# Weight-summing transfers in pairs behind eight of the attention's weight tiles, instead of one behind each of 30 tiles and two in the next stage

## The chip, the core and the metric

One core of a Trainium2 chip runs the kernel. The core has five engines, each with an in-order queue of its own: TensorE (PE in the profile; its weight loads are PEld), VectorE (DVE), ScalarE (ACT), GpSimd (POOL) and SyncE (SP). Sixteen DMA engines move data between the large memory and the core's on-chip memory; SP issues almost all transfers of this kernel and POOL the ones that this change moves. The metric is the time of one execution on the device in microseconds (us), lower is better; the median over several runs counts.

## What is computed

One layer over 512 latent tokens of width 1024 with 256 context tokens. A modulated norm, one wide input projection, and from its columns two mixers side by side: a bidirectional Mamba-2 SSD scan with 32 heads in 4 groups, and windowed attention with 16 query heads on 4 key heads. Both are projected, gated and merged, and a gated ConvFFN follows.

```python
h_lat = modulate(x, norm1_g, sh1, sc1);  p_lat = h_lat @ w_in
y_l = ssd_bidir(...)                      # chunks of 128 tokens, both directions
att_lat = window_ctx_attention(q, k, v, k_ctx, v_ctx, sink)
out = (g_ssd * (ssd @ w_o_ssd) + g_att * (att @ w_o_att)) @ w_out
x = x + gt1 * out
u = dwconv_centred(modulate(x, norm2_g, sh2, sc2) @ w_up, ...)
x = x + gt2 * ((silu(u[:, :D_FF]) * u[:, D_FF:]) @ w_down)
return rmsnorm(x, final_g)
```

All is float32. Each product of matrices is made of three faster ones: both operands are split into a high part and a low part (a rounded copy and the rest), and high by high, high by low and low by high are added up.

## The kernel before

**Stages.** In order: modulation and the first projections (until about 88 us of the profile), attention (to about 366), the SSD scan (to about 700), the output projections, the ConvFFN. PE runs matmuls in all of them.

**Weight tiles.** A weight tile is 128 x 1024 (512 KB). `load_raw` (L172) lets SP load it into one of three `raw` buffers (tile `wraw` in the profile). It is then split: ACT copies it rounded into `whi`, DVE subtracts into `wlo`; of each there are two buffers. In `split` (L178, L179) this is done for the stages that go through `run`, which loads one tile ahead. In the attention it is done by `high` (L1078) and `low` (L1081) inside `product_atoms`: a planner orders the attention's work, and beside the attention proper 30 weight tiles (the list `BESIDE`, numbered g from 0) are multiplied to fill PE: query and key projections, gates `z` of the SSD (written away at L1118), and parts of the attention's output projection (L1067 to L1069, written away at L1109). `high` of tile g also issues the load of tile g + 1, which waits until the split of the tile that held the buffer is done.

**Queries and keys.** A query tile is made into the operands of the scores by `q_low` (L878, L880): the low part lands in a `tc` buffer (two in all, shared with `out_low` at L1003), and three transfers of SP copy half-tiles within the on-chip memory. The last waits for the first. Scores are at L948; for each block ACT takes exponentials (L964), PE transposes (L984), ACT and DVE split (L988, L992), PE multiplies by the values (L997).

**Start of the SSD stage.** The attention's end also makes decay tables. They are written to the large memory (`cs_d`, `tt_d`) and read back spread over all partitions: `tb` (L1241), from which ACT makes `eT` (L1286), and `fb` (L1565, 512 KB each, eight per group of heads, four buffers), from which ACT makes `E` (L1584). The stage's own weight tiles have key `x`. The first gives BT after a short convolution (L1381 on ACT, L1382 and L1383 on DVE, L1389 on ACT, L1390 on DVE), and PE transposes BT at L1409 after it has multiplied the second tile.

**The weight sums.** The ConvFFN's last product works with sums of blocks of `w_down`. They are made ahead of time by transfers alone: `SUMS` is a list of 32 transfers of 704 KB (tile `dsum`), from the large memory to itself, four plain copies and then four that add to what the copies wrote, and this four times over; two of the four copying groups read what an earlier group summed. `sum_step` (L155 to L160) issues the next one from POOL and makes it wait for the DVE instruction that it is given, the low part of a split. It is called for every tile of the attention by `low` (L1079 to L1081) and, while the list lasts, for the `x` tiles by `load` (L198 to L200). POOL's other work in the attention is nil; its first work of the SSD stage comes after 425 us. The sums are read in the ConvFFN only.

Of the kernel before, what the change touches and what calls it, by code (L numbers as in the profile page):

```python
# [13 lines left out]
ALU = mybir.AluOpType  # L14
# [25 lines left out]
def raw(ap):  # L40
    return ap.bitcast(F32)
# [3 lines left out]
def tile_hybrid_layer(  # L45
# [31 lines left out]
    V, S, G, T = nc.vector, nc.scalar, nc.gpsimd, nc.tensor  # L77
# [69 lines left out]
    SUMS = []  # L147
# [4 lines left out]
        SUMS += [(DSUMS[j][q], more[q], dict(accum_op=ALU.add, max_dma_last_dim=DK * P)) for q in range(4)]  # L152
    BEHIND = mybir.DependencyInfo(mybir.DependencyClass.Sync, mybir.DependencyReason.DATA)

    def sum_step(ins):  # L155

        if SUMS:
            o, x, how = SUMS.pop(0)
            dma = G.dma_start(o, x, **how)  # L159
            tc.add_manual_dep(dma.ins, ins.ins.name, BEHIND, reason="weight sums behind a split")  # L160
# [3 lines left out]
    def load_raw(key):  # L164
        a, n = src[key]
        if key[0] == "dn" and key[1] >= 4 and key[1] % 2:
            if "dnraw" not in F:
                F["dnraw"] = hpool.tile([P, 5, 6 * P], F32, tag="hlh", name="dnraw")
            r = F["dnraw"][:, key[1] // 2 % 5, :]
        else:  # L170
            r = wpool.tile([P, 1024], F32, tag="raw", name="wraw", bufs=3)
        dma = nc.sync.dma_start(r[:, :n], a)  # L172
        if key[0] == "m":
            M_LOADS[key[1]] = dma
        return r, n

    def split(r, n, hi, lo):
        S.copy(hi[:, :n], r[:, :n])  # L178
        return V.tensor_tensor(lo[:, :n], r[:, :n], raw(hi[:, :n]), ALU.subtract)  # L179
# [3 lines left out]
    def load(key):  # L183
        r, n = load_raw(key)
        if key[0] == "m":
            return r
        if key in ELSEWHERE:
            hi, lo = ELSEWHERE[key]()
            split(r, n, hi, lo)
            return hi, lo  # L190
        if key[0] == "dn" and key[1] % 4 > 1:
            if "dnw" not in F:
                F["dnw"] = hpool.tile([P, 2, 2, 6 * P], F32R, tag="hll", name="dnw")
            hi, lo = (F["dnw"][:, key[1] % 2, i, :] for i in range(2))
        else:
            hi = wpool.tile([P, 1024], F32R, tag="whi", name="whi", bufs=2)
            lo = wpool.tile([P, 1024], F32R, tag="wlo", name="wlo", bufs=2)
        low = split(r, n, hi, lo)  # L198
        if key[0] == "x":
            sum_step(low)  # L200
        return hi, lo

    def run(prog, early=None):

        seq = [k for keys, _ in prog for k in keys]
        have, nload, nuse = {}, 0, 0
        for keys, fn in prog:
            nuse += len(keys)
            ahead = 1 + (early in keys) + any(k[0] == "dn" for k in keys)
            while nload < min(nuse + ahead, len(seq)):  # L210
                have[seq[nload]] = load(seq[nload])
                nload += 1
            fn(*[have.pop(k) for k in keys])
# [102 lines left out]
    class Plan:  # L316
# [6 lines left out]
        def add(self, name, engine, cost, needs, rank, emit, whole=True, load=0.11, late=False):  # L323


            self.atoms[name] = dict(
                name=name, engine=engine, cost=cost, needs=needs, rank=rank, emit=emit, whole=whole, load=load,
                late=late, start=None,
            )
# [86 lines left out]
    with tc.tile_pool(name="spool", bufs=1) as sp:  # L416
# [235 lines left out]
        r = {}  # L652
        cq = tmp("te")[:, :LC]
        for j in range(KT):
# [46 lines left out]
            x = ("hi", "lo") if j >= NU else ("hh", "hl")  # L701
# [31 lines left out]
        for n in range(2):  # L733
            for j in range(KT):
                x = ("hi", "lo") if j >= NU else ("hh", "hl")
# [319 lines left out]
    def product_atoms(g, key, accs):  # L1055

        kind, t = key
        d, R, G_ = {}, 1e6 + 100 * g, "%d" % g
# [19 lines left out]
            S.copy(d["w"][0], d["r"])  # L1078

        def low():  # L1080
            sum_step(V.tensor_tensor(d["w"][1], d["r"], raw(d["w"][0]), ALU.subtract))  # L1081

        def rope_part(f):
            scale = -0.125 if kind == "k" else 1.0
# [37 lines left out]
        rw = R - 2e6 if g != 1 else -500  # L1122
        atom("w" + G_, "ACT", 1.05, was, rw, high, late=g > OLD)
        atom("v" + G_, "DVE", 1.225, ["w" + G_], rw, low, late=g > OLD)
        ks = range(-4 if kind == "k" else 0, 8)
        for k in ks:
# [1054 lines left out]
```

## Time and profile before

| | |
|---|---|
| median of 3 runs | 1239.54 us (1237.92 to 1241.78) |
| the profiled execution | 1237.59 us, span 1235.8 us |
| PE, DVE, ACT, POOL busy | 99%, 75%, 55%, 14% of the span |
| transfers issued by SP | 94736 packets, 181.32 MB, 46.7% of the time of 16 DMA engines |
| transfers issued by POOL (the weight sums) | 8960 packets, 23.07 MB, 8.3% |
| mean granted PE clock | 0.994 of full speed |

The span is what the profiler saw of the execution, from its first instruction to its last. Times inside the profile are counted from the span's start. A row of an order of time gives start, length, engine, line, operation, what is written from what, and in brackets how long the engine had idled and what released it. A row of waits gives who waited for whom, the sum, the number of times and the longest. "DMA to landing" is the time from the issue of a transfer to its last byte.

### The profile page before, as it was taken

What the parts mean: (1) busy time and instruction counts of PE and PEld (TensorE: products, weight loads), DVE (VectorE), ACT (ScalarE), POOL (GpSimd) and SP (SyncE); (2) the same over time, 40 slices, a digit from 0 to 9 for tenths busy, and PEclk for the clock granted to TensorE, in tenths of its full rate; (3) what the DMA queues carried; (4) which work ended last, traced back from release to release, by engine and by line L of the source; (5) the groups of instructions that cost most, each with busy time, mean ns of one, the idle gap of its engine ahead of it and who ended that gap; (6) DMA issues with size and microseconds to landing.
All of it is one profiled execution on the core that took longest, in us unless ns stands there. A gap on an engine that the chain in (4) does not pass through costs nothing.

```text
span 1235.8 us, 18429 instructions
## 1 busy us (share of the span) xinstructions
PE 1222.6 (99%) x6790; PEld 1023.5 (83%) x6790; DVE 921.5 (75%) x1518; ACT 685.8 (55%) x1289; POOL 170.6 (14%) x177
## 2 busy tenths in 40 slices
PE   9999999999998999999999999999999999999997
PEld 6798888888877877778777778889988888889997
DVE  5857788888554688697896768667777877778785
ACT  5658788787444457476575663223634344345662
POOL 0000000100110043262451631000200000000000
PEclk9999999999998999999999999999999999999998
DMA  9645585745798346346356568676133433337662
GB/s 361 259 135 185 108 219 162 155 150 139 206 244 197 107 117 164 127 124 200 97 172 197 173 206 266 229 244 208 51 108 115 136 104 117 112 106 235 186 178 82
DMA packets 104761, 206.35 MB, mean 167 GB/s; under 512 B 8928, under 2 KB 52768, under 8 KB 104416
## 3 DMA queue, kind: packets, MB, share of 16 engines
q1 hardware_dynamic: 94736, 181.32, 46.7%
q0 software_dynamic: 8960, 23.07, 8.3%
q8 instruction: 53, 0.87, 0.3%
q10 hardware_dynamic: 976, 0.79, 0.2%
q14 instruction: 36, 0.29, 0.1%
HBM read 182.54 MB, written 40.17 MB: 180 GB/s over the span
## 4 chain that ended last, share of the span: by engine, by line
PE 96%; DMA 2%; DVE 1%; ACT 1%; issue 0%; SPq 0%; POOL 0%; DVEq 0%; ACTq 0%; POOLq 0%
PE acc L230 19%; PE acc L233 19%; PE acc L231 19%; PE score L948 3%; PE po L997 3%; PE pt L984 2%; PE mis L570 2%; PE mis L1601 2%; PE mis L1494 2%; PE acc L1973 2%; PE acc L1975 2%; PE acc L1974 2%; PE mis L1609 1%; PE mis L1974 1%; PE mis L1973 1%; PE mis L1975 1%
## 5 line engine op out<-in xcount | busy, mean ns | idle before, releaser
L178 ACT CAST whi<-wraw 128x1024 fp32r<-128x1024 f32 (+3 forms) x118 | 120.0, 1018 | 151.0 <-PE acc L231 111.8
L230 PE MATMUL acc<-hlh,whi 128*128 128x512 f32 x472 | 195.0, 413 | 0.0
L179 DVE TENSOR_TENSOR wlo<-wraw,whi 128x1024 fp32r<-128x1024 f32 (+3 forms) x118 | 142.9, 1211 | 66.5 <-ACT whi L178 64.1
L231 PE MATMUL acc<-hll,whi 128*128 128x512 f32 x472 | 185.7, 394 | 0.0
L233 PE MATMUL acc<-hlh,wlo 128*128 128x512 f32 x472 | 185.6, 393 | 0.1
L230 PE MATMUL acc<-mh,whi 128*128 128x512 f32 x368 | 143.3, 390 | 0.0
L233 PE MATMUL acc<-mh,wlo 128*128 128x512 f32 x368 | 143.2, 389 | 0.0
L231 PE MATMUL acc<-ml,whi 128*128 128x512 f32 x368 | 143.2, 389 | 0.0
L233 PEld LDWEIGHTS acc<-hlh,wlo 128*128 128x128 f32 x472 | 89.0, 188 | 20.4 <-DVE wlo L179 0.8
L230 PEld LDWEIGHTS acc<-hlh,whi 128*128 128x128 f32 x472 | 89.4, 189 | 18.0 <-issue 3.1
L231 PEld LDWEIGHTS acc<-hll,whi 128*128 128x128 f32 x472 | 89.4, 189 | 17.5 <-issue 2.4
L230 PEld LDWEIGHTS acc<-mh,whi 128*128 128x128 f32 x368 | 69.1, 188 | 14.4
L233 PEld LDWEIGHTS acc<-mh,wlo 128*128 128x128 f32 x368 | 69.1, 188 | 14.4
L231 PEld LDWEIGHTS acc<-ml,whi 128*128 128x128 f32 x368 | 69.1, 188 | 14.2
L284 POOL TENSOR_TENSOR rs<-ms,phalf 128x2 f32<-128x2 f32 (+1 forms) x5 | 4.8, 954 | 463.8 <-DVE ms L283 463.8
L1382 DVE SCALAR_TENSOR_TENSOR ta<-acc,half,ta 128x511 f32<-128x511 f32 (+1 forms) x66 | 43.9, 665 | 32.7 <-ACT ta L1381 32.4
L957 DVE CUSTOM_DVE_ANT_0 p<-score,winm,nsink 128x512 f32<-128x512 f32 (+1 forms) x64 | 51.8, 810 | 15.4 <-PE score L948 13.9
L964 ACT ACTIVATE p<-p,mneg 128x512 f32<-128x512 f32 (+1 forms) x64 | 49.7, 777 | 15.4 <-DVE mneg L957 14.8
L1381 ACT ACTIVATE ta<-acc,half 128x512 f32<-128x512 f32 (+1 forms) x66 | 46.8, 709 | 19.8 <-PE acc L233 18.6
L230 PE MATMUL acc<-hch,whi 128*128 128x256 f32 x176 | 54.7, 311 | 0.0
L159 POOL DMA_DIRECT2D dsum<-wdn x24 | 20.7, 861 | 241.0 <-DVE wlo L1081 222.4
L992 DVE TENSOR_TENSOR ptl<-pt,pth 128x512 fp32r<-128x512 f32 x72 | 47.5, 685 | 8.5 <-ACT pth L988 7.7
(414 smaller groups left out, 3186.9 us busy)
## 6 DMA issues: line engine op xcount, KB each, us to landing
wraw<-wup SPq DMA_DIRECT2D x44, 512.0 KB, 3.6
dsum<-wdn POOLq DMA_DIRECT2D x24, 704.0 KB, 7.9
fb<-cs_d SPq DMA_DIRECT2D x32, 512.0 KB, 6.5
wraw<-wm SPq DMA_DIRECT2D x32, 512.0 KB, 4.0
wraw<-wx SPq DMA_DIRECT2D x24, 512.0 KB, 3.7
wm<-wm SPq DMA_DIRECT2D x16, 512.0 KB, 8.3
wraw<-wz SPq DMA_DIRECT2D x16, 512.0 KB, 4.2
wraw<-wos SPq DMA_DIRECT2D x16, 512.0 KB, 4.9
```

The costliest lines, as they stand in the source:

```text
L178: S.copy(hi[:, :n], r[:, :n])
L179: return V.tensor_tensor(lo[:, :n], r[:, :n], raw(hi[:, :n]), ALU.subtract)
L230: T.matmul(ps, wh, xh[:, k0 + k, :], start=a, stop=False)
L231: T.matmul(ps, wh, xl[:, k0 + k, :], start=False, stop=False)
L233: T.matmul(ps, wl, xh[:, k0 + k, :], start=False, stop=b)
L948: T.matmul(ps[:, o : o + len(z) * P], Q[h][:, b * P : (b + 1) * P], k[:, j, z[0] * P : (z[-1] + 1) * P], start=v == 0 and o % 512 in (0, P ...
L957: V.tensor_tensor_reduce(p[:, :w], d["ps"][i][:, o0 : o0 + w], m, op0=ALU.add, op1=ALU.min, scale=1.0, scalar=nsink[:, h : h + 1], accum_o ...
L964: S.activation(p, p, AF.Exp, bias=d["mneg"][:, i : i + 1], scale=-1.0, accum_out=d["den"][:, i : i + 1])
L992: V.tensor_tensor(d["ptl"][x], d["pt"][x], raw(d["pth"][x]), ALU.subtract)
L997: T.matmul(d["po"], vst[:, cols[x], j, :], d[y][x], start=x == 0 and y == "pth", stop=x == c - 1 and y == "ptl")
L1381: S.activation(o[:, :n], ps[:, :n], AF.Identity, scale=hcol(base_w, stride + i), bias=hcol(base_b, i))
L1382: V.scalar_tensor_tensor(o[:, 1:n], ps[:, 0 : n - 1], hcol(base_w, i), o[:, 1:n], ALU.mult, ALU.add)
```

## The change

`sum_step` can issue several transfers behind one instruction. Tiles 4 to 11 of the attention carry two each, all others one, and the `x` tiles of the SSD stage carry none: 4 + 16 + 12 = 32, so the list is used up with tile 23. No transfer is added or removed, and their order stays.

```diff
-    def sum_step(ins):
-
-        if SUMS:
+    def sum_step(ins, n=1):
+
+        for _ in range(min(n, len(SUMS))):
             o, x, how = SUMS.pop(0)
             dma = G.dma_start(o, x, **how)
             tc.add_manual_dep(dma.ins, ins.ins.name, BEHIND, reason="weight sums behind a split")
...
-        low = split(r, n, hi, lo)
-        if key[0] == "x":
-            sum_step(low)
+        split(r, n, hi, lo)
         return hi, lo
...
         def low():
-            sum_step(V.tensor_tensor(d["w"][1], d["r"], raw(d["w"][0]), ALU.subtract))
+            sum_step(V.tensor_tensor(d["w"][1], d["r"], raw(d["w"][0]), ALU.subtract), 1 + (4 <= g < 12))
```

Lines behind L200 stand two lines earlier in the kernel after.

## The prediction

> **What bounds the kernel now.** I read the engine table of the page first, then the waits of TensorE, then TensorE's order of time at its longest wait, then the chain of waits back from there.
>
> ```profile
> PE 1222.6 (99%) x6790; PEld 1023.5 (83%) x6790; DVE 921.5 (75%) x1518; ACT 685.8 (55%) x1289; POOL 170.6 (14%) x177
> ...
> PE mis L1409 <- DVE BT L1390: 4.0, 1, 4.0
> ```
>
> TensorE (PE) works for 1222.6 of 1235.8 us, so a change that removes no matmul can gain only what PE loses to waits and to a lower clock. Of its waits one is long: L1409, the first transposes of the SSD stage, waits 4.0 us for the tile BT from VectorE (DVE). PE around it:
>
> ```profile
> 379.71 0.39 PE L233 MATMUL acc<-hlh,wlo 128*128 128x512 f32 x1
> 384.10 1.12 PE L1409 MATMUL mis<-ident,BT 128*128 128x128 f32 x4 [4.00 <-DVE BT L1390]
> ...
> 388.87 0.52 PE L233 MATMUL acc<-hlh,wlo 128*128 128x512 f32 x1
> 389.23 0.39 PE L230 MATMUL acc<-hlh,whi 128*128 128x512 f32 x1
> 389.46 0.39 PE L231 MATMUL acc<-hll,whi 128*128 128x512 f32 x1
> ...
> 262.74 1.31 PE pt L984 x12
> ```
>
> Matmuls follow each other every 0.23 us at full pace (389.23 to 389.46), so the last one before the wait gives way at 379.94. From there to 389.23 there are 4 transposes and 9 matmuls to do (three rounds of L230, L231, L233). Twelve transposes take 1.31 us in the chain, 0.11 each. Undisturbed: 4 x 0.11 + 9 x 0.23 = 2.5 us. It took 389.23 - 379.94 = 9.3. **The place costs 6.8 us**: 4.16 of waiting (to 384.10), 2.64 of slow work after it. The table by stretches (stretch and its length, busy us of PE, PEld, DVE, ACT, POOL, then granted clock, DMA share, GB/s) says why the work is slow:
>
> ```profile
> 381.30:384.10 2.80, 0.00 (x0) 0.00 (x1) 2.01 (x4) 1.41 (x3) 0.00 (x0) 0.68 1.14 254
> 384.10:388.20 4.10, 4.03 (x11) 2.92 (x12) 1.95 (x3) 0.77 (x2) 0.00 (x0) 0.50 0.90 208
> ...
> 366.00:380.00 14.00, 14.00 (x74) 11.79 (x72) 1.23 (x1) 3.62 (x10) 2.03 (x2) 1.00 1.08 242
> ```
>
> The clock falls during the wait (0.68 over 381.30 to 384.10 is full clock for 1.0 us, then half, so at 382.3, 2.4 us into it) and is 0.50 until 388.2 at least. Before it, from 366 to 380, the DMA engines are full (share 1.08). The chain of waits that ends there, in order of time (start, us, what):
>
> ```profile
> 355.22 7.90 DMA tb<-tt_d
> 363.47 1.04 ACT whi L178
> ...
> 366.18 11.71 DMA fb<-cs_d
> ...
> 377.92 2.45 ACT E L1584 x8
> 380.37 0.67 ACT ta L1381
> ...
> 383.35 0.69 DVE BT L1390
> ...
> 384.88 1.22 DVE wlo L179
> ```
>
> ScalarE (ACT) is an in-order queue: the E work of the SSD's first chunk stands ahead of the convolution L1381 that BT comes from. E waits for fb, a load that needs 11.71 us to land. While it travels, ACT and DVE idle and PE uses up its lead. What fills the DMA engines are the weight sums. POOL's order of time shows their issues, two answers on line L159 the landings of the last two, and an answer on line L1565 what the later fb loads need:
>
> ```profile
> 351.69 1.07 POOL L159 DMA_DIRECT2D dsum<-wdn  x1 [5.64 <-DVE wlo L1081]
> 358.23 1.03 POOL L159 DMA_DIRECT2D dsum<-wdn  x1 [5.46 <-DVE wlo L1081]
> 366.06 1.01 POOL L159 DMA_DIRECT2D dsum<-wdn  x1 [6.81 <-DVE wlo L179]
> 369.04 1.02 POOL L159 DMA_DIRECT2D dsum<-wdn  x1 [1.97 <-DVE wlo L179]
> ...
> DMA to landing us min/median/max: 13.6/13.6/13.6
> ...
> DMA to landing us min/median/max: 15.8/15.8/15.8
> ...
> L1565 SPq DMA_DIRECT2D fb<-cs_d x27: 359/385/840, 447.6 to 690.7; - x27
> ...
> DMA to landing us min/median/max: 5.2/6.4/9.5
> ```
>
> The four last sums accumulate. Two are issued beside fb, at 366.06 and 369.04, and land after 13.6 and 15.8 us. The 27 fb loads after 395 us, with no sum about, land in 5.2 to 9.5 us, median 6.4.
>
> **The change, part by part.** On every engine the instructions keep their order; only the waits of POOL's transfers change. There are 32: four plain copies, four accumulating ones, four times over. Before, one goes behind each of the 30 attention tiles and two behind the first two tiles of the SSD stage. After, tiles 0 to 3 and 12 to 23 carry one each, tiles 4 to 11 two each: 16 + 16 = 32.
>
> *Removed at the end.* The eight transfers issued from 328.7 us on move forward; the last of the 32 now goes behind tile 23, at 325.93 before. Issued there it lands near 335 (325.93 and the 9.3 us of an accumulating one, quoted below), and from then on none is about. If fb is issued at 366.18 as now and takes the median 6.4, it lands at 372.6. BT followed the landing by 384.04 - 377.89 = 6.15 us, so it is ready at 378.7, before PE asks at 379.94. The wait goes, and with it the slow clock. The next in line is the split of the third weight tile, whose low part ended at 386.10, 2.06 us after BT: now 380.8. PE asks for it after 4 transposes and two matmuls, at 379.94 + 0.44 + 0.46 = 380.84. That fits with nothing to spare, but there is a second shift:
>
> ```profile
> 360.30 0.39 PE L1069 MATMUL acc<-khi,wlo 128*128 128x512 f32 x1
> ```
>
> fb is issued behind the fourth SSD weight load on SP's queue, that load behind the low part of the first tile's split, that behind ACT's cast (363.47), and that behind tb, a load of 128 KB that needed 7.90 us beside two sums. The cast's buffer is free when PE ends the last tile but one (row above, next tile from 360.54), so the cast can go up to 2.9 us earlier, and fb with it. Between 0 and 2.9 I need none for the forecast; whatever comes of it is spare.
>
> *Moved forward.* From tile 12 on the sequence is the old one eight places early, and of the same kind at each tile (plain for plain); the new load lies at tiles 4 to 11, where before POOL issued:
>
> ```profile
> 124.32 1.10 POOL L159 DMA_DIRECT2D dsum<-wdn  x1 [8.76 <-DVE wlo L1081]
> 137.11 1.02 POOL L159 DMA_DIRECT2D dsum<-wdn  x1 [11.69 <-DVE wlo L1081]
> ...
> 173.42 0.52 POOL L159 DMA_DIRECT2D dsum<-wdn  x1 [8.13 <-DVE wlo L1081]
> 179.53 0.50 POOL L159 DMA_DIRECT2D dsum<-wdn  x1 [5.60 <-DVE wlo L1081]
> ...
> DMA to landing us min/median/max: 9.3/9.3/9.3
> ```
>
> An accumulating one lands after 9.3 us (that of 137.11). After: two accumulating at 124.3, two at 137.1, then two plain twice (156.3 and 164.3, where accumulating ones stood), two accumulating at 173.4 and two more at 179.5 (plain before), then plain pairs at 191.8 and 200.9. The dense place is 173 to some 197: a first landing at 182.7, the next three each 5.2 us on (369.04 + 15.8 less 366.06 + 13.6), 198.3 at most. POOL has nothing else here, so its own extra waits cost nothing. What counts is which load from SP's queue is late. Weight loads, the copies that build the queries, and who needs them:
>
> ```profile
> L172 SPq DMA_DIRECT2D wraw<-wz x1: 1874/1874/1874, 177.8 to 177.8; - x1
> ...
> 198.27 1.04 ACT L1078 CAST whi<-wraw 128x1024 fp32r<-128x1024 f32 x1
> ...
> L880 SPq DMA_DIRECT2D q<-tc x1: 462/462/462, 177.3 to 177.3; - x1
> ...
> 184.85 0.58 ACT L1003 COPY tc<-po 64x512 f32<-64x512 f32 x1 [1.70 <-PE po L997]
> ...
> L880 SPq DMA_DIRECT2D q<-tc x2: 462/464/467, 198.8 to 200.0; - x2
> ...
> DMA to landing us min/median/max: 2.2/2.3/2.7
> ...
> 207.29 0.28 PE L948 MATMUL score<-khi,q 128*128 128x256 f32 x1
> ```
>
> Weight loads are issued three tiles ahead: that of 177.8 is cast at 198.27, 20 us later, so even a landing as slow as the slowest sum's 15.8 us is in time. The query copy of 177.3 holds a tc buffer that ACT writes again at 184.85: 7.5 us. The copy of 200.0 feeds the score at 207.29: 7.3 us, of which 2.7 were used. So I take 0 for the attention; the bounds are 0 and what the second and third rival cost. Below zero is out: PE is busy without a gap there (PE's only long wait is the one above).
>
> [...]
>
> **Sum.** Against the profiled execution, 1235.8 of span in 1237.59 us: -4.16 - 2.64 + 0 = -6.8, a span of 1229.0 in 1230.8 us. The median of the runs, 1239.54, lies 1.95 above that execution; I keep the distance: 1239.54 - 6.8 = **1232.7 us**. A change within 0.3% (3.7 us, so 1235.8 to 1243.3) cannot be told from none here; -6.8 is 0.55%.
>
> **The rivals.** *fb stays late by itself (0.12).* From 366.18 with the worst 9.5 it lands at 375.7, BT at 381.8: PE waits 1.9. With the clock at full, as it was 1.9 us into the old wait, the gain is 4.9, 1234.6 us; with the slow work of before as well it is 4.9 - 2.64 = 2.3, 1237.2. For it: five such loads follow at once and share the engines. Against: the first goes first. [...]
>
> *The query copies at 200 come late (0.08)*: gain and loss cancel.
>
> ```profile
> DMA to landing us min/median/max: 2.2/2.7/7.3
> ```
>
> The worst of all query copies took 7.3. The last one is issued once its forerunner (197.6) has landed: 197.6 + 7.3 + 7.3 = 212.2, 4.9 after the score wants it, with the 2.64 of slow clock 7.5: 1239.54 - 6.8 + 7.5 = 1240.2. Against: by 197 only plain copies are left, and beside those this copy took 2.7 at most.
>
> *Slower (0.14)*: the copy of 177.3 gets through only behind the queued sums at tiles 8 and 9. ACT then stands at L1003 from 184.85 until 193.1 to 198.3 (third or fourth landing), 8.2 to 13.4 us, with exponentials and transposed scores behind it on its queue and PE behind those. With 2.64 for the clock and the 6.8 gained: 1243.6 to 1248.8; it decides from a hold of 4.2 us on. For it: fb did starve beside two sums. Against: the copy is small, its worst landing (7.3) would end at 184.6, and that case had an accumulating sum over it since 164.3, which is now a plain pair, so the copy will be issued before the sums of 173.4 get going.
>
> **How the numbers follow.** Forecast 0.66 (its own range 1231.1 to 1235.0: the runs' 1237.92 to 1241.78 less 6.8), rivals 0.12, 0.08, 0.14. Faster: 0.66 and half of the first rival (the other half I leave to the lower clock), 0.72. Same: its other half and most of the second, 0.13. Slower: 0.15. The range runs from 1 us below the forecast's lower end to the second rival, 1230.0 to 1240.5, leaving out the third and a little of the rest.
>
> **What would show it.** Right: no wait of PE at L1409, clock 1.00 throughout 366 to 400, fb of the first chunk landing within 5.2 to 9.5 us, tb well under 7.9, POOL's last sum near 326 us, PE without a gap from 85 to 380. First rival: L1409 still waits, 1 to 3 us. Second: PE waits at a score near 207. Third: ACT idle at L1003 on a DMA near 185. The forecast is wrong if the wait at L1409 stays with no sum on the way, or if PE shows a new gap in the attention.

## The result, and the profile after

| | median | runs | lowest to highest | ratio to the kernel before, with its 95% interval |
|---|---|---|---|---|
| before | 1239.54 us | 5 | 1237.92 to 1241.78 | |
| after | 1232.03 us | 5 | 1229.70 to 1234.24 | 0.9936, 0.9916 to 0.9955 |
| after once more, in the third group below | 1231.58 us | 5 | 1231.35 to 1232.64 | 0.9931, 0.9917 to 0.9944 |

The kernel after is faster by 7.5 us (0.6%) where 6.8 were forecast. The profiled execution after took 1229.70 us, its span 1227.9 against 1235.8. The engine table and the waits of TensorE in it:

```profile
PE 1218.8 (99%) x6790; PEld 1021.5 (83%) x6790; DVE 921.4 (75%) x1518; ACT 686.7 (56%) x1289; POOL 170.0 (14%) x177
```

```profile
PE mis L288 <- POOL rs L282: 1.1, 1, 1.1
PE mis L446 <- DVE ones L429: 1.0, 1, 1.0
PE mis L271 <- ACT tc L2073: 0.8, 1, 0.8
```

The wait for BT, 4.0 us before, is gone (the three that are left are the same as before, near the start and the end). PE is also busy for 3.8 us less, with the same 6790 matmuls. The stretches show where most of that comes from (columns as in the prediction):

```profile
366.00:380.00 14.00, 14.00 (x77) 12.08 (x76) 5.85 (x8) 8.16 (x19) 0.00 (x0) 1.00 0.82 216
...
381.30:384.10 2.80, 2.80 (x14) 2.27 (x13) 2.01 (x4) 0.79 (x2) 0.00 (x0) 1.00 0.63 237
384.10:388.20 4.10, 4.10 (x32) 3.91 (x31) 1.88 (x3) 1.50 (x3) 0.00 (x0) 1.00 0.06 22
```

The clock is 1.00 throughout, and 384.10 to 388.20 holds 32 matmuls, most of them half as wide, where it held 11. The DMA engines are not full from 366 to 380 (0.82, before 1.08). ScalarE's order of time at the place:

```profile
357.95 0.42 ACT L1284 ACTIVATE eT<-tb 128x256 f32<-128x256 f32 x1 [1.94 <-DMA tb<-tt_d]
359.88 1.05 ACT L178 CAST whi<-wraw 128x1024 fp32r<-128x1024 f32 x1 [1.51 <-PE acc L1066]
...
368.82 2.45 ACT L1582 ACTIVATE E<-fb,TX 128x128 f32<-128x128 f32 x8 [1.85 <-DMA fb<-cs_d]
```

The first cast of the SSD stage (L178) now waits for PE and not behind tb, 3.59 us earlier than before (363.47); fb is issued earlier with it, and the E work starts at 368.82 instead of 377.92. How much of the span belongs to this place follows from two markers on PE in each execution, a score in the attention and a group of transposes (L1409, L1407 after) beyond the place. Before, then after:

```profile
203.56 0.28 PE L948 MATMUL score<-khi,q 128*128 128x256 f32 x1
...
403.00 0.60 PE L1409 MATMUL mis<-ident,tc 128*128 128x128 f32 x4
```

```profile
202.86 0.28 PE L946 MATMUL score<-khi,q 128*128 128x256 f32 x1
...
395.55 0.60 PE L1407 MATMUL mis<-ident,tc 128*128 128x128 f32 x4
```

Between them lie 199.44 us before and 192.69 after: 6.75 us. Another 0.70 lies ahead of the first marker, all of it in the first 20 us (the matmul that starts at 20.0 us before starts 0.74 us earlier after), and the remaining 0.45 of the 7.9 behind the second. The 0.70 does not need the change: the first sum of all is issued at 92.2 us in this execution of the kernel before, and between 91.3 and 92.1 in other executions of kernels that do the same up to there.

### The profile page after: what moved, and what is told of

Its sections match the earlier page's. It is cut to its first block, busy times and chain, and to the rows that moved or that the text cites. A ratio compares the mean times of both kernels' runs of the same rounds, so it can differ in the third digit from the quotient of the medians.

```text
span 1227.9 us, 18427 instructions
## 1 busy us (share of the span) xinstructions
PE 1218.8 (99%) x6790; PEld 1021.5 (83%) x6790; DVE 921.4 (75%) x1518; ACT 686.7 (56%) x1289; POOL 170.0 (14%) x177
## 4 chain that ended last, share of the span: by engine, by line
PE 99%; DVE 0%; ACT 0%; issue 0%; POOL 0%; DVEq 0%; ACTq 0%; POOLq 0%
PE acc L228 20%; PE acc L231 20%; PE acc L229 20%; PE score L946 3%; PE po L995 3%; PE pt L982 2%; PE mis L568 2%; PE mis L1599 2%; PE mis L1492 2%; PE acc L1971 2%; PE acc L1973 2%; PE acc L1972 2%; PE mis L1607 1%; PE mis L1972 1%; PE mis L1971 1%; PE mis L1973 1%
## 5 line engine op out<-in xcount | busy, mean ns | idle before, releaser
L178 ACT CAST whi<-wraw 128x1024 fp32r<-128x1024 f32 (+3 forms) x118 | 120.0, 1018 | 156.4 <-PE acc L229 112.1
L784 DVE SCALAR_TENSOR_TENSOR tm<-wraw,csil,tm 128x512 f32<-128x512 f32 x56 | 44.4, 793 | 12.4 <-DMA wraw<-wm 11.3
```

The source lines that it names most:

```text
L784: V.scalar_tensor_tensor(acc, r[:, u * 512 : u * 512 + 512], sc, acc, ALU.mult, ALU.add)
```

## The experiments

Three groups of four kernels each; the kernels of one group ran on one chip beside the kernel before (medians 1239.28, 1238.73 and 1240.47 us). Each ratio goes by the kernel before of its own group, so kernels of different groups are compared by their ratios. The first group takes the change apart.

**The last two transfers alone.** Their old places behind the first two tiles of the SSD stage are freed. To make room, the transfers behind tile 4 move forward by up to two places, so tiles 26 to 29 carry the last four, all accumulating, where tiles 26 and 27 carried plain ones before.

```diff
-            sum_step(V.tensor_tensor(...), 1 + (4 <= g < 12))
+            sum_step(V.tensor_tensor(...), 1 + (4 <= g < 6))
```

> The kernel after with pairs behind attention tiles 4 and 5 only: the list ends with tile 29, the last two transfers leave the two first tiles of the SSD stage and nothing else of the old order is kept off (two accumulating transfers still go near 351 and 358 us). Theory (fb starves beside the two transfers issued after 366 us): these two alone carry the gain; fb is issued near 366, lands after some 6 to 8 us, PE waits 0 to 0.5 us at the transposes of BT, the clock is 1.00 from 366 to 400: 1232 to 1234.5 us, ratio 0.993 to 0.996. Rival 1 (the early loads tb decide: they were late beside the transfers at 351.7 and 358.2, which are kept here): tb still needs near 8 us, PE waits 1.5 to 4 us and the time is 1236 to 1239.5. Rival 2 (the gain of the change lies in the attention's denser order or in the start of the execution, not in this place): no wait of 4 us at the place, and yet 1237 to 1239.5.

Measured: 1236.66 us (9 runs, 1233.23 to 1237.48), ratio 0.9971 (0.9960 to 0.9983). The chain of waits and PE's waits:

```profile
346.31 5.43 DMA cs_d<-du
...
351.75 6.80 DMA tt_d<-tt
...
358.62 7.93 DMA tb<-tt_d
...
366.90 1.04 ACT whi L178
...
369.60 6.46 DMA fb<-cs_d
```

```profile
PE acc L228 <- ACT whi L178: 2.2, 1, 2.2
```

fb lands in 6.46 us, as the theory wants, and yet more than half of the gain is missing. The time is lost ahead of fb: the tables are written late (cs_d, tt_d), tb is late behind them, the first cast starts at 366.90, and PE waits for that cast. Rival 1, the early loads, has both the number and the place. But the accumulating sums at tiles 26 and 27 (issued at 339.38 and 345.02, landed after 9.9 and 12.9 us; the plain ones before landed after 6.1 and 5.6) may be part of why the tables are late, so this run does more than free the last two. The next one does only that.

**The same, with the two moved behind later tiles of the SSD stage** (in the kernel before):

```diff
-        if key[0] == "x":
+        if key[0] == "x" and key[1] not in (16, 20):
```

> The kernel before with the last two transfers put behind two later weight tiles of the SSD stage instead of the first two; all 30 tiles of the attention keep one each. Theory (it is the time of those two transfers beside fb, not that they stand in the SSD stage or that others stand earlier): the wait at BT goes to under 0.5 us, 1232 to 1234.5 us. Rival 1 (tb decides): 1236 to 1239.5. Rival 3 (later loads of the SSD stage suffer in the same way, so what is gained at the first chunk is lost at the next): a new PE wait of 2 to 4 us after 390 us, 1236 to 1240.

Measured: 1233.09 us (1232.52 to 1235.17), ratio 0.9956 (0.9944 to 0.9969). Time and the wait for BT are as the theory has them; but in the profiled execution, the slowest of the five, PE waits 3.1 us for the first cast, for the same reason as in the run above (tb issued at 361.06, cast at 367.80). No new wait comes behind 390 us, so rival 3 falls.

**The earlier places alone.** Six pairs in the attention, nothing between tile 23 and the SSD stage, the last two transfers where they were.

```diff
-            sum_step(V.tensor_tensor(...))
+            sum_step(V.tensor_tensor(...), (1 + (4 <= g < 10)) * (len(SUMS) > 2))
```

> The other part of the change alone: six pairs in the attention, so that no transfer goes between tile 23 and the SSD stage, but the last two of the list stay behind the first two tiles of the SSD stage. Theory (fb starves beside those two): tb lands in 3 to 5 us, fb is issued up to 3 us earlier than before (363 to 366) but still needs 9 to 12 us, PE waits 1 to 4 us at BT and the clock may still fall: 1235 to 1239.5 us. Rival 1 (tb and the early cast decide): tb in 3 to 5 us, no wait at BT, 1232 to 1234.5. Rival 2 (the gain lies in the attention): 1232 to 1234.5 with a wait of 2 us or more still there.

Measured: 1230.90 us (1230.15 to 1231.76), ratio 0.9935 (0.9924 to 0.9947): the whole gain, with the two transfers that were to be its cause still in place. POOL's and ScalarE's order of time:

```profile
362.88 1.01 POOL L159 DMA_DIRECT2D dsum<-wdn  x1 [36.18 <-DVE wlo L179]
368.77 1.03 POOL L159 DMA_DIRECT2D dsum<-wdn  x1 [4.88 <-DVE wlo L179]
```

```profile
359.07 0.42 ACT L1286 ACTIVATE eT<-tb 128x256 f32<-128x256 f32 x1 [2.67 <-DMA tb<-tt_d]
360.28 1.05 ACT L178 CAST whi<-wraw 128x1024 fp32r<-128x1024 f32 x1 [0.79 <-PE acc L1068]
...
369.90 2.46 ACT L1584 ACTIVATE E<-fb,TX 128x128 f32<-128x128 f32 x8 [2.53 <-DMA fb<-cs_d]
```

One sum is issued just ahead of fb (362.88, fb at 363.00), the second 5.8 us later, and fb lands after 6.9 us. So "the two sums issued beside fb starve it" cannot be the whole cause. Rival 1 has the mechanism (tb after 4.5 us, no wait at BT); the time is 1.1 us below its range.

**The last two as plain copies**, at their old places. The last addition into two blocks of the sums is left out.

```diff
+    SUMS[-2:] = [(o, x, {}) for o, x, _ in SUMS[-2:]]
```

> The kernel before with the last two of the 32 transfers as plain copies: the last addition is left out of two blocks of the sums, so the output differs. Places, sizes and order stay. Theory (an accumulating transfer starves the loads, a plain copy of the same bytes hardly does): fb lands in 6 to 8 us, PE waits under 1 us at BT: 1232 to 1235 us. Rival (any transfer of 704 KB beside fb costs the same, by its bytes): fb still needs 10 us or more, the wait stays 3 to 4 us: 1238 to 1240.

Measured: 1240.33 us (12 runs), ratio 1.0011 (1.0001 to 1.0021); the wait for BT is 4.0 us. The chain of waits:

```profile
359.35 6.38 DMA tb<-tt_d
...
368.78 11.03 DMA fb<-cs_d
```

Two plain copies beside fb (issued at 368.66 and 370.09) hold it for 11.03 us, as the accumulating ones did for 11.71. That they accumulate does not decide.

These four left a new theory, the chain: the decay tables pass through four transfers in a row, written (cs_d, tt_d), tb read, fb read, and a delay in each adds up against a room of a few us. The second group tests it, and the terms that the prediction put at nothing.

**Two transfers late in the attention, none later.**

```diff
-            sum_step(V.tensor_tensor(...), 1 + (4 <= g < 12))
+            sum_step(V.tensor_tensor(...), 0 if 24 <= g < 28 else 1 + (4 <= g < 10))
```

> Six pairs at tiles 4 to 9, so 30 transfers are issued by tile 23; the last two, accumulating, go behind tiles 28 and 29 (near 351 and 358 us), as two accumulating ones did before; tiles 24 to 27 and the first tiles of the SSD stage carry none. Chain theory (formed after the first four runs: the tables go through four transfers in a row, cs_d and tt_d written, tb read, fb read, and each of them is slowed by whatever sum is then on the way): the tables are written in some 2 to 3 us, tb takes 6 to 8 us, fb 6 to 8 us; BT is late by 0 to 2.5 us: 1232 to 1235.5 us, between the kernel after and the one that only frees the first tiles of the SSD stage (1236.66). Old theory (only transfers beside fb matter): 1231 to 1233. If tb decides alone: 1235.5 to 1237.5.

Measured: 1230.14 us (1229.87 to 1230.72), ratio 0.9929 (0.9917 to 0.9942). ScalarE's order of time, and PE's only new wait:

```profile
363.34 1.03 ACT L178 CAST whi<-wraw 128x1024 fp32r<-128x1024 f32 x1
...
372.77 2.46 ACT L1582 ACTIVATE E<-fb,TX 128x128 f32<-128x128 f32 x8 [5.57 <-DMA fb<-cs_d]
```

```profile
PE acc L231 <- DVE wlo L179: 0.4, 1, 0.4
```

tb is late, the cast too (363.34, as late as before), fb starts late and lands in 6.7 us, all as the chain theory says; only the price was put too high, because the room takes it: 0.4 us of wait is left. The time lies below all three ranges and nearest to that of the old theory, so it is tb and the cast, and not the time, that speak for the chain here. E starts 3.95 us later than after (368.82) and costs almost nothing, so the room is about that large.

**Double density in the attention.** Four transfers behind each of tiles 4 to 11.

```diff
-            sum_step(V.tensor_tensor(...), 1 + (4 <= g < 12))
+            sum_step(V.tensor_tensor(...), 4 * (4 <= g < 12))
```

> All 32 transfers behind tiles 4 to 11, four behind each (none behind tiles 0 to 3), so all are issued by 201 us and POOL's queue holds up to four sums at a time. Theory (the attention has slack for loads of 10 us and more late, at twice the density of the change too): no new PE wait over 0.5 us between 90 and 366 us, 1230 to 1233 us. Rival (the query copies or weight loads come late: ACT held at L1001, or a score waits): a PE wait of 3 us or more between 125 and 230 us, 1235 to 1246.

Measured: 1234.36 us (1232.77 to 1236.32), ratio 0.9962 (0.9950 to 0.9974). It is the rival's mechanism, at less than its price (a wait of 2.3 us where it had 3 or more, and a time between the two ranges):

```profile
PE score L946 <- DMA q<-tc: 2.3, 1, 2.3
```

The last query copy (issued at 204.25, landed after 5.3 us) is late for the score, as the prediction's second rival has it. Nothing is held at L1001 (ACT's copy into `tc`, L1003 before).

**No sums in the attention at all**; they go behind the ConvFFN's first 32 tiles.

```diff
-        split(r, n, hi, lo)
+        low = split(r, n, hi, lo)
+        if key[0] == "up":
+            sum_step(low)
...
-            sum_step(V.tensor_tensor(...), 1 + (4 <= g < 12))
+            sum_step(V.tensor_tensor(...), 0)
```

> No transfer in the attention at all: the 32 go behind the first 32 tiles of the ConvFFN's first product, one each. A bound for what the sums still cost the attention and the start of the SSD stage after the change. If the attention pays nothing for them (the prediction's cost of 0): 1230 to 1233 us, the same as after. If it still pays: 1226 to 1230. If the ConvFFN has less slack for them than the attention: a new PE wait behind 900 us and 1233 to 1240.

Measured: 1233.30 us (6 runs, 1231.36 to 1235.84), ratio 0.9956 (0.9945 to 0.9968). The two markers:

```profile
203.29 0.28 PE L948 MATMUL score<-khi,q 128*128 128x256 f32 x1
...
395.97 0.60 PE L1409 MATMUL mis<-ident,tc 128*128 128x128 f32 x4
```

Between the markers lie 192.68 us without any sum and 192.69 in the profiled execution after. But the pairs (124 to 201 us) lie ahead of the first marker. A score that starts at 119.28 us before, at 118.58 after and at 119.01 here lies ahead of them: from it to the first marker all three need 84.28 us. So in these profiles neither stretch pays anything for the sums. What this kernel pays lies in the ConvFFN: against the profiled execution of before it loses 2.4 us between 900 and 1100 us; waits for three low parts make up 1.1 of them. The cause of the spread of its other runs is open.

**The clock alone.** In the kernel before, 18 matmuls whose result is not used go ahead of the transposes of BT.

```diff
+            if g == 0:
+                warm = misb()
+                for _ in range(18):
+                    tc.keep_in_program_order(T.matmul(warm, hlh[:, 0, :P], hlh[:, 0, :], start=True, stop=True))
```

> The kernel before with 18 matmuls of 128x512 put on TensorE ahead of the first transposes of BT; what they compute is not used. They take 18 x 0.23 = 4.1 us, as much as the wait, and keep TensorE busy in it, so that only the slow work after the wait goes. If the prediction's split holds (4.16 us of wait, 2.64 us of slow clock): clock 1.00 after the wait, 1236 to 1238 us. Rival (the slow clock costs nothing by itself, because BT's followers are late anyway): 1239 to 1241.

Measured: 1240.68 us (11 runs, 1237.21 to 1243.12), ratio 1.0012 (1.0002 to 1.0023); no gain. VectorE's and PE's order of time in the profiled execution (span 1235.7):

```profile
380.79 0.69 DVE L1390 SCALAR_TENSOR_TENSOR BT<-tb,ta 128x512 f32<-128x512 f32 x1 [0.76 <-ACT tb L1389]
```

```profile
381.88 4.25 PE L1439 MATMUL mis<-hlh 128*128 128x512 f32 x18
```

Here tb was late (cast at 366.08) and PE waited 1.2 us for the first cast. But fb, issued at 368.78, landed after 6.54 us, and BT was ready at 381.48, before PE came to the added matmuls. So this execution had no wait for BT that they could fill: they stand in for nothing and cost their 4.25 us. The clock is 1.00 from 384.10 to 388.20, in an execution with no wait over 1.2 us at this place. PE's busy time (1224.5 us) less the added work is 1220.2 us, 2.4 below before; that is near the 2.64 of slow work, but any execution without the slow stretch would show it. How the price splits into wait and clock therefore rests on the rows of the kernel before alone; this profile does not test it. The median lies in the rival's range, and why the other executions are no faster is open.

The third group asks whether the delays add up, and whether the pairs at tiles 10 and 11 cost something.

**Both late groups together.**

```diff
-            sum_step(V.tensor_tensor(...))
+            sum_step(V.tensor_tensor(...), 0 if 24 <= g < 28 else 1 + (4 <= g < 8))
```

> Four pairs at tiles 4 to 7, one each at the others up to tile 23, none at tiles 24 to 27, one each at tiles 28 and 29 and at the two first tiles of the SSD stage: the last four transfers of the kernel before (all accumulating) at their old places, the four ahead of them moved forward. Either half alone was free (1230.14 us with the two at tiles 28 and 29, 1230.9 us with the two in the SSD stage). Chain theory (the delays of tb and fb add up, and the room of some 4 us takes one of them but not both): tb lands late, fb too, BT late by 2 to 4 us, and the time goes back to 1236 to 1239.5 us. Rival (the queue of eight behind each other is what starves the tables; four are handled): 1230 to 1233.5.

Measured: 1238.62 us (11 runs, 1236.38 to 1239.47), ratio 0.9982 (0.9973 to 0.9991). Either half alone gave 0.993; together most of the gain is lost again. The chain of waits, and PE's wait:

```profile
350.80 3.32 DMA tt_d<-tt
354.19 7.08 DMA tb<-tt_d
...
364.32 13.68 DMA fb<-cs_d
```

```profile
PE mis L1409 <- DVE BT L1390: 4.3, 1, 4.3
```

tb is only 2.6 us slower than in the run that keeps the last two and frees the rest (7.08 against 4.5), but fb needs 13.68 us instead of 6.9, with the same two transfers issued around it. The sum of 358.02 (landed after 9.1 us) is still on the way beside the one of 364.20. So the delays do more than add up.

**Four in a row at tiles 26 to 29.**

```diff
-            sum_step(V.tensor_tensor(...), 1 + (4 <= g < 12))
+            sum_step(V.tensor_tensor(...), 0 if 24 <= g < 26 else 1 + (4 <= g < 8))
```

> Four pairs at tiles 4 to 7, none at tiles 24 and 25, one each at tiles 26 to 29 (four accumulating ones, from about 338 us on), none in the SSD stage: the same four transfers, 13 us earlier than in the run with two at tiles 28 and 29 and two in the SSD stage. Chain theory: the writes of the tables and tb are late (tb issued near 358, landed near 366), the first cast of the SSD stage is then late for TensorE by 1 to 3 us, fb itself lands in 6 to 8 us: 1232.5 to 1237 us. Rival (only what is on the way beside fb and tb counts, the two transfers ahead of them are gone by then): 1230 to 1232, as with two.

Measured: 1234.76 us (1233.83 to 1236.86), ratio 0.9956 (0.9943 to 0.9968). The chain of waits, and PE's wait:

```profile
353.07 8.72 DMA tt_d<-tt
361.87 5.61 DMA tb<-tt_d
...
367.82 1.04 ACT whi L178
```

```profile
PE acc L228 <- ACT whi L178: 3.2, 1, 3.2
```

The same four transfers some 12 us earlier hit the tables' writing instead of fb, and PE waits for the first cast instead of BT.

**Six pairs, the list done with tile 25**, and **the kernel after once more**:

```diff
-            sum_step(V.tensor_tensor(...), 1 + (4 <= g < 12))
+            sum_step(V.tensor_tensor(...), 1 + (4 <= g < 10))
```

> The kernel after with six pairs instead of eight: none at tiles 10 and 11, the list ends with tile 25 (near 338 us). Theory (the two runs with six pairs agreed within 1.6 us, the kernel after ranged over 4.5 us; its pairs at tiles 10 and 11 sometimes make the query copies near 200 us late for the score at 207 us): 1229.5 to 1231, all runs within 1.5 us. Rival (the sums near 332 and 338 us reach the tables again): 1232 to 1235.

> The kernel after once more, beside the same runs of the kernel before as the other three: 1230 to 1234 us. If the spread comes from the query copies, some profile of it shows a wait of up to 3 us at the score near 207 us; otherwise there is no PE wait over 1.1 us.

Measured: six pairs 1229.83 us (4 runs, 1229.69 to 1230.14), ratio 0.9914 (0.9900 to 0.9927); after 1231.58 us, ratio 0.9931 (0.9917 to 0.9944). The intervals overlap, but the two ran on the same chip, and there the slowest run with six pairs (1230.14) is faster than the fastest of after (1231.35). The profiled execution of after shows a wait that fits (order of time of SP, POOL and PE):

```profile
199.47 1.79 SPq L1116 DMA_DIRECT2D zs_d<-te  x1
200.33 0.96 POOL L159 DMA_DIRECT2D dsum<-dsum  x2 [8.06 <-DVE wlo L1079]
201.95 0.46 SPq L878 DMA_DIRECT2D q<-tc  x1
...
208.38 0.36 PE L946 MATMUL score<-khi,q 128*128 128x256 f32 x1 [1.46 <-DVE wlo L1079]
```

SP is held at a store for 1.79 us, the last query copy goes out at 201.95, needs 6.3 us and lands at 208.25; the score starts at 208.38 after 1.46 us of wait. (The bracket names the low part wlo, which the score does not read; the copy is what came last.) With one sum at this tile the copy is issued here and lands after 2.6 us:

```profile
199.64 0.46 SPq L878 DMA_DIRECT2D q<-tc  x1
```

On this chip six pairs are 1.75 us faster than the kernel after.

## Why the prediction was right, and where it was not

The chain in all kernels, from the profiled execution of each (tb and fb: issued at, landed after; "cast" is the start of the first L178 of the SSD stage; "MB" is what POOL's queue, which carries the sums, moved while fb was on its way):

| kernel | tb | cast | fb | MB | PE waits | median |
|---|---|---|---|---|---|---|
| before | 355.22, 7.9 | 363.47 | 366.18, 11.7 | 1.00 | 4.0 for BT | 1239.54 |
| added matmuls | 358.63, 7.1 | 366.08 | 368.78, 6.5 | 0.16 | 1.2 cast | 1240.68 |
| plain last two | 359.35, 6.4 | 366.08 | 368.78, 11.0 | 1.44 | 1.8 cast, 4.0 BT | 1240.33 |
| both late groups | 354.19, 7.1 | 361.61 | 364.32, 13.7 | 1.28 | 4.3 for BT | 1238.62 |
| last two freed | 358.62, 7.9 | 366.90 | 369.60, 6.5 | 0.02 | 2.2 cast, 1.0 low parts | 1236.66 |
| four at tiles 26 to 29 | 361.87, 5.6 | 367.82 | 370.51, 6.1 | 0 | 3.2 cast | 1234.76 |
| four at each of tiles 4 to 11 | 357.89, 3.2 | 362.97 | 365.69, 5.3 | 0 | 2.3 at a score near 209 | 1234.36 |
| sums in the ConvFFN | 354.16, 4.0 | 360.30 | 363.02, 5.9 | 0 | none here | 1233.30 |
| last two later | 361.06, 6.4 | 367.80 | 370.49, 6.2 | 0 | 3.1 cast | 1233.09 |
| last two kept, rest early | 354.57, 4.5 | 360.28 | 363.00, 6.9 | 0.13 | none | 1230.90 |
| two at tiles 28, 29 | 357.39, 5.6 | 363.34 | 366.04, 6.7 | 0.11 | 0.4 | 1230.14 |
| after | 354.37, 3.6 | 359.88 | 362.60, 6.2 | 0 | none | 1232.03 |
| after once more | 356.51, 3.8 | 361.67 | 364.39, 6.1 | 0 | 1.5 at a score near 208 | 1231.58 |
| six pairs | 353.77, 3.9 | 359.81 | 362.53, 6.1 | 0 | none | 1229.83 |

*The price of the place, 6.8 us.* Right: 6.75 between the markers. Wait and clock both went, as forecast (no wait at BT, clock 1.00).

*The cause.* Right in kind: fb took 11.7 us beside the sums and 6.2 after, beside none, and E, the convolution and BT came behind fb. Too narrow in its place: the prediction put it on the two sums issued at 366.06 and 369.04. Taking these two away gives 0.9956 to 0.9971 of the time, not 0.9936, and keeping them and moving the six before them gives it all. It takes the sums of 351.69 and 358.23 as well; with both groups fb is back at 13.7 us and the kernel near its old time. Nor is it enough that the two are issued beside fb: in the kernel with added matmuls they go out at 368.66 and 370.43, fb at 368.78, and fb lands after 6.5 us, because they move only 0.16 MB meanwhile. That accumulating sums are the ones that starve loads was a guess too: plain ones did the same.

*The second shift.* The step "Between 0 and 2.9 I need none for the forecast; whatever comes of it is spare" is the one that failed. Its sum holds: with fb issued at 366.04 and landed after 6.7 us (two at tiles 28, 29) PE waits 0.4 us. What does not hold is the issue time "as now". The two runs that free the SSD stage's first tiles and keep the sums ahead of them gain 2.6 and 6.2 us where 7.5 came. In the profiled execution of before, tb was issued at 355.22; in the three kernels with the same transfers up to tile 29 (plain last two, last two later, added matmuls) it was issued at 358.6 to 361.1, and there the first cast itself came too late for PE, by 1.2 to 3.1 us. The prediction took one execution's chain for the chain; with fb issued near 370, a landing in 6.4 us does not save the place. The forecast came out right, in part by luck, because the change frees both ends.

*The attention at nothing.* Right in the first profile, where the stretch with the pairs takes the same 84.28 us as before and as without any sum. In the second profile of after it costs 1.46 us, and six pairs show it can be avoided. This is the second rival's mechanism in full: the query copy of 200 us, late for the score at 207. The prediction argued it away with "beside those this copy took 2.7 at most". That was with one plain sum issued 0.85 us behind it. With a pair issued at the same time it took 5.8 us in the first profile after (landed 206.0, in time), and with a pair issued 1.6 us ahead of it 6.3 in the second. The rival's own price, 7.5 us, was too high, since only the last copy is slowed so much, and it leaves the gain at the place whole.

*The slower rival.* It did not come about. As the prediction argues, the copy goes out (at 174.22) before the two sums of that tile, issued at 172.72 and 173.37, have moved anything, and it lands after 6.2 us, in time. But ACT does not wait for this copy at all: with four sums at a tile it is issued at 180.42 and lands at 186.57, 1.8 us after ACT has begun to write `tc`, and ACT's wait is for PE alone:

```profile
184.76 0.58 ACT L1001 COPY tc<-po 64x512 f32<-64x512 f32 x1 [1.70 <-PE po L995]
```

So the link from this copy to ACT, and the 7.5 us that the prediction takes from it as a bound, are not borne out. Which of the two `tc` buffers each of them uses, the rows do not say.

*fb late by itself.* Not so: 5.3 to 6.9 us in every kernel in which the sums moved at most 0.16 MB while it was on its way. Which end its 1.9 us of wait would have, 1234.6 at full clock or 1237.2 with the slow work, and so the half of it counted as faster, was the author's estimate. After PE's waits of 1.8 and 2.2 us for the first cast (plain last two, last two freed) the clock is 1.00 over 366 to 380.

## What to carry to other kernels

Here background transfers that are needed only in the ConvFFN cost 7.5 us (1239.54 against 1232.03) where a chain of dependent transfers ran, written tables read back in two steps. In a case like it, look for the whole chain, add up how late each link may be, and count every link that the background touches, not only the one that the profile names last: either late group alone was nearly free (ratios 0.9929 and 0.9935), and both together cost most of the gain (0.9982). One profiled execution shows one way in which such a chain is late, so a second execution, or the lowest and highest of the runs, belongs beside it. And when transfers are bunched elsewhere, look at the copies with the least time to their use: here pairs were free at six tiles of the attention, and in one of two profiled executions not at the two that run beside a query copy with some 7 us to go (it took 6.3 us, and PE waited 1.46).

## What the runs showed of the hardware

**fb was slow where the sums moved much beside it, not wherever they were issued beside it.** In the runs with the last two kept and with both late groups a sum is issued 0.12 us ahead of fb. What POOL's queue (q0) then moved until fb had landed (packets, MB, share of the time of 16 DMA engines), in this order:

```profile
q0 software_dynamic: 93, 0.13, 21.1%
```

```profile
q0 software_dynamic: 941, 1.28, 62.1%
```

fb took 6.9 and 13.7 us. Over all kernels (the column "MB" above) it took 5.3 to 6.9 us beside at most 0.16 MB of the sums, and 11.0 to 13.7 us beside 1.00 to 1.44 MB, whether plain or accumulating. A longer flight meets more of them in any case, but it is also 0.09 to 0.13 MB in each us against 0.03 at most. In the run with the last two kept, the sum issued at 362.88 had hardly begun when the first fb landed; the second fb, issued at 368.60, met 1.41 MB of the sums and took 13.95 us, where it took 6.46 after, beside none. In the run with both late groups the sum of 358.02 was on the way until 367.1, beside fb from 364.32 on; in the run with the last two kept POOL had issued none for 36 us before 362.88. What this did to fb is not shown.

From 372 to 381 us of the kernel before, with sums and SP's loads both on the way, POOL's queue moved 1.08 MB and SP's 1.01. How the engines share their time between the two queues is not shown.

**SP's own issue took longer too.** The issue of the first fb took 0.45 us before and after. The next four fb took 16.43 us to issue before, with sums on the way, and 6.35 after, with none (the longest single one 7.66 and 2.72 us):

```profile
369.24 16.43 SPq L1565 DMA_DIRECT2D fb<-cs_d  x4
```

```profile
368.20 6.35 SPq L1563 DMA_DIRECT2D fb<-cs_d  x4
```

The weight load that follows on SP's queue was issued at 386.12 before and at 377.03 after.

**Where PE waited 3.1 us or more, the clock was low, for about 3.4 or 6.8 us where the rows show its end.** With a wait of 2.2 us (last two freed) the clock stayed at 1.00. With 3.2 us (four at tiles 26 to 29, PE idle from 365.7 to 368.9) it is low after the wait is over:

```profile
369.00:370.00 1.00, 0.75 (x2) 0.19 (x2) 1.00 (x1) 1.00 (x2) 0.00 (x0) 0.68 0.00 0
370.00:371.00 1.00, 0.84 (x2) 0.75 (x3) 0.79 (x2) 0.76 (x2) 0.00 (x0) 0.50 0.68 262
371.00:372.00 1.00, 1.00 (x3) 0.74 (x3) 0.53 (x1) 0.00 (x0) 0.00 (x0) 0.50 0.81 106
372.00:373.00 1.00, 1.00 (x4) 0.82 (x3) 0.00 (x0) 0.00 (x0) 0.00 (x0) 0.61 0.97 344
```

The lowest rows here show 0.50. Counted as time at 1.00 and at 0.50, a stretch of 1 us at mean clock c has 2 x (1 - c) us at 0.50: 0.64 + 1 + 1 + 0.78 = 3.42 us in all. In the kernel before, where the wait is 4.0 us, the same count from these two rows and the six at 0.50 between them gives 0.68 + 6 + 0.14 = 6.82, twice as much:

```profile
382.00:383.00 1.00, 0.00 (x0) 0.00 (x0) 0.60 (x1) 0.31 (x1) 0.00 (x0) 0.66 1.13 229
...
389.00:390.00 1.00, 1.00 (x6) 0.83 (x5) 0.42 (x1) 1.00 (x3) 0.00 (x0) 0.93 1.23 325
```

After 3.1 us (last two later: 0.59 and 0.71 over the two ends, 0.50 over the 2 us between) it gives 3.40. After 4.3 us (both late groups: 0.83 over 381.30 to 384.10, 0.50 to 388.20, 0.52 over 389 to 390, the 0.8 us between the last two taken at 0.50) it gives 6.81. After 4.0 us in plain last two the clock is 0.50 over 389 to 390, and its rise is not in the rows.

The clock fell 2.4 us into the wait before, but 3.7 us from its start in four at tiles 26 to 29, so the time since the start of the wait alone does not say when it falls. Between the 2.2 us without a slow stretch and the 3.1 us with one these rows show nothing.
